# A feed-forward chunk's products grouped by width, two head groups' values issued together, and two longer distances, in a two-layer decoder trunk on one core

## The chip, the cores and the metric

The kernel runs on one core of a Trainium2 chip. The metric is the device time of one execution in microseconds (us), taken over several runs; one further execution is profiled. Five engines work side by side, each through its own queue: TensorE (PE; its weight loads are listed apart as PEld), VectorE (DVE), ScalarE (ACT), GpSimd (POOL), and SyncE (SP), which issues most DMA transfers.

## What is computed

The reference is a decoder trunk of two layers over 256 tokens of width 1024. Cut to what matters here:

```
for layer in range(2):
    x = x + 0.5 * swiglu_ffn(rms_norm(x), w_gu, w_down)      # feed-forward, width 2816
    x = x + mixer(rms_norm(x))                               # layer 0: even, layer 1: odd
    x = x + memory_cross_attention(rms_norm(x), rms_norm(mem))
    x = x + 0.5 * swiglu_ffn(rms_norm(x), w_gu2, w_down2)

def swiglu_ffn(x, w_gu, w_down):
    gate, up = jnp.split(x @ w_gu, 2, axis=-1)
    return (jax.nn.silu(gate) * up) @ w_down
```

The even mixer has eight heads of banded attention (window 128, sinks) and eight of stick-breaking attention; the odd mixer has sixteen heads whose scores get a table of distances added before the softmax. Both work with heads of 64 elements. The cross-attention has four heads of 256 over 256 memory tokens. All of it is float32.

## The kernel before

**Products.** Every weight tile of 128 x 1024 float32 elements (512 KB) is loaded into a buffer `raw`, and split into a high part `wh` (a ScalarE cast, L175) and the rest `wl` (a VectorE subtraction, L177); activations are split in the same way (`split_to`, L190 and L191). A product is then the sum of three matmuls in PSUM: high x high, high x low, low x high (`mm3`, L182 to L184). There are 10 buffers each of `wh` and `wl`, 4 of `raw`, and PSUM has 6 banks for sums (`mm`) and 2 for transposes (`tp`).

**Feed-forward.** The 2816 hidden columns are worked through in 11 chunks of 256. A chunk needs four weight tiles, and gives two results, gate and up, of 256 features x 256 tokens each. `ws_wide` makes one of the two: the weights are the stationary operand, and two banks are filled, each in eight steps over the width. A step is one matmul of 512 columns (`wh` against the high and the low half of the activations side by side, L323) and one of 256 columns (`wl` against the high half, L324), both into the same bank. ScalarE copies the second half of the bank out (L327) and VectorE adds it to the first (L328). `silu` and the product of the two results follow, and the chunk's features are split for the down projection. The first feed-forward makes chunk 0 otherwise (`ws_blocks`) and chunks 1 to 10 with `ws_wide`; the three later ones make chunks 0 and 1 token by token with `mm3` and chunks 2 to 10 with `ws_wide`. So 37 chunks, each of 32 pairs of a wide and a narrow matmul, go through it: 1184 pairs.

**The order of the attention work.** Attention is threaded between the matmuls of other projections by a clock of its own: every stretch of matmuls adds its estimated time (`tick`), and work put off with `later(delay, ...)` is issued as soon as that clock has passed its due time. The delays stand in `LAG`. `norm` is the distance from a token block's normalisation on VectorE (L231) to its transposes on TensorE; `x_p` that from the scaling of the cross-attention's weights (L452) to theirs. Where the program needs a result (`need(tag)`), what is left under that tag is issued at once. The framework under it may still move an instruction past its neighbours.

`attend` runs the attention of a list of head groups: `one(i)` makes the scores and the exponentials of group i, `share` (L452) divides by the sum, `two` transposes the weights (four transposes into a `tp` bank, L212) and copies them to SBUF (VectorE, L481), and after `LAG['pv']` `values` multiplies them with the values (L496: pairs of matmuls on one half of the output rows each). There are 6 groups in the even mixer and 12 in the odd one.

Of the kernel before, what the change touches and what calls it, by code (L numbers as in the profile page):

```python
# [27 lines left out]


LAG = {  # L30
    "norm": 5000, "silu": 5000, "pv": 3000, "head256": 2200, "band": 7500, "band_gap": 2600, "band_p": 7500,
    "put": 400, "att_norm": 4500, "band_norm": 3500, "stick_gap": 1900, "stick_u": 3200, "stick_v": 1000, "stick_o": 1300, "head64": 7000,
    "att_first": 3800, "att_gap": 3300, "att_p": 17600, "att_o": 1800, "x_s": 18000, "x_p": 4000, "x_out": 3600,
    "mem_e": 5400, "mem_o": 4600, "rs64": 2700, "rs256": 1900, "rsband": 6100,
}

# [2 lines left out]
def kernel(  # L39
# [52 lines left out]
    def later(delay, fn, tag=None):  # L92
        serial[0] += 1
        heapq.heappush(heap, (clock[0] + delay, serial[0], tag, fn))
# [8 lines left out]
    def tick(ns):  # L103
        clock[0] += ns
        if heap and not busy[0] and heap[0][0] <= clock[0]:
            dispatch()
# [40 lines left out]
    def psum():  # L147
        return mm.tile([P, 512], F32, name="mm")
# [7 lines left out]
    def work(dt=F32):  # L156
        return wk.tile([P, 512], dt, name="wk")
# [28 lines left out]
    def cols(w, o, n):  # L186
        return w[0][:, o:o + n], w[1][:, o:o + n]
# [123 lines left out]
                mm3(ps[:, b * 256:(b + 1) * 256], cols(w[k // per], o, P), xboth(k), k == 0, k == NK - 1)  # L311
                tick(330)

    def ws_wide(w, g):


        part, out = work(), work()
        for b in range(2):
            ps = psum()
            for k in range(NK):  # L320
                o = (k % 2) * 512 + g * 256 + b * P
                wh, wl = cols(w[k // 2], o, P)
                nc.tensor.matmul(ps, lhsT=wh, rhs=xs[:, :, :, k, :], start=k == 0, stop=False)  # L323
                nc.tensor.matmul(ps[:, 0:256], lhsT=wl, rhs=xh[:, :, k, :], start=False, stop=k == NK - 1)  # L324
                tick(347)
            bs = slice(b * 256, (b + 1) * 256)
            nc.scalar.copy(part[:, bs], ps[:, 256:512])  # L327
            nc.vector.tensor_tensor(out[:, bs], ps[:, 0:256], part[:, bs], op=ALU.add)  # L328
        return out


    def start(load):
# [25 lines left out]
    def ffn(w_gu, w_down, next_vec, first=False):  # L358
# [44 lines left out]
        for c in range(0 if first else 2, NF // 2):  # L403
            w = ws[0] if first and c == 0 else load_chunk(c)
            if first and c == 2:
                announce(next_vec, kept=True)
            if first and c == 0:
                pg = psum()
                ws_blocks(pg, w[0], 0, 4, by_pass=True)
                pu = psum()  # L410
                ws_blocks(pu, w[1], 0, 4)
            else:
                pg = ws_wide(w, 0)
                pu = ws_wide(w, 1)
            s = work()
            nc.scalar.activation(s, pg, AF.Silu)
            h = work()
            nc.vector.tensor_tensor(h, pu, s, op=ALU.mult)
            dh, dl = hslot(c)
            split_to(dh, dl, blocks(h, 256))  # L420
# [34 lines left out]
    def attend(groups, scores, values, gap, norm, wait, first=0.0, tag=None, ready=None):  # L455

        def one(i):
            p, nm, sink = scores(groups[i])
            n, keys = p.shape[1], p.shape[2]
            dn = sm.tile([P, 4], F32, name="dn")
            for j in range(n):
                nc.scalar.activation(p[:, j, :], p[:, j, :], AF.Exp, bias=nm[:, j:j + 1], accum_out=dn[:, j:j + 1])
            p = p.rearrange("p a b -> p (a b)")
            if sink is not None:
                nc.scalar.activation(sink, sink, AF.Exp)

            def share():
                if sink is not None:
                    nc.vector.tensor_tensor(dn[:, 0:n], dn[:, 0:n], sink, op=ALU.add)
                nc.vector.reciprocal(dn[:, 0:n], dn[:, 0:n])
                scale_heads(p, p, dn, keys)
            later(norm, share, tag)

            def two():
                ps = transpose4(p)
                pt = work()  # L480
                nc.vector.tensor_copy(pt, ps)  # L481
                if ready is None:
                    later(LAG['pv'], lambda: values(groups[i], pt), tag)
                else:
                    ready(groups[i], lambda: later(LAG['pv'], lambda: values(groups[i], pt), tag))
            later(wait, two, tag)
            if i + 1 < len(groups):
                later(gap, lambda: one(i + 1), tag)
        later(first, lambda: one(0), tag)
# [395 lines left out]
    class Memory:  # L885
# [11 lines left out]
        def values(self, arrived):  # L897

            self.v = [(slot(F32R), slot(F32R)) for _ in range(2)]

            def evac(t, c, ps):
                split_to(*[d[:, c * 512:(c + 1) * 512] for d in self.v[t]], ps)
                if t == 1:
                    arrived(c)
            project(lambda k: self.w[k * P:(k + 1) * P, 1024:2048], self.parts, evac)
# [148 lines left out]
```

## Time and profile before

| | |
|---|---|
| time, three runs | 1203.28, 1199.79, 1201.71 us; median 1201.71 |
| the profiled execution's own time | 1202.92 us |
| its span, first to last instruction | 1201.2 us |
| TensorE busy | 1189.3 us, 99% of the span |
| VectorE busy, ScalarE busy | 775.1 us (65%), 646.5 us (54%) |
| granted TensorE clock, mean | 0.999 of full speed |
| DMA | 216.70 MB, 180 GB/s |

The profiled execution took 1.7 us more than its span, before the first and after the last instruction. A row of the timeline gives the start, the duration, the engine, the line and the operation with its shapes, and in brackets how long the engine had been idle before and on whom it waited. Durations of matmuls overlap those of the next one, so that how long a matmul occupies TensorE is read from the distance between two starts, not from its duration. The clock of TensorE has two levels, 1.2 and 2.4 GHz; 1.00 in a row means 2.4.

### The profile page before, as it was taken

What the parts mean: (1) busy time and instruction counts of PE and PEld (TensorE: products, weight loads), DVE (VectorE), ACT (ScalarE), POOL (GpSimd) and SP (SyncE); (2) the same over time, 40 slices, a digit from 0 to 9 for tenths busy, and PEclk for the clock granted to TensorE, in tenths of its full rate; (3) what the DMA queues carried; (4) which work ended last, traced back from release to release, by engine and by line L of the source; (5) the groups of instructions that cost most, each with busy time, mean ns of one, the idle gap of its engine ahead of it and who ended that gap; (6) DMA issues with size and microseconds to landing.
All of it is one profiled execution on the core that took longest, in us unless ns stands there. A gap on an engine that the chain in (4) does not pass through costs nothing.

```text
span 1201.2 us, 16964 instructions
## 1 busy us (share of the span) xinstructions
PE 1189.3 (99%) x6320; PEld 998.7 (83%) x6320; DVE 775.1 (65%) x1026; ACT 646.5 (54%) x1080; POOL 63.9 (5%) x123
## 2 busy tenths in 40 slices
PE   8999999999999999999999999999999999999998
PEld 7888888986788888888888888888777888888887
DVE  6766645696777676665375765376786676667651
ACT  6656534665565466555265564265764564655540
POOL 1000000200110000000000000032000100000000
PEclk9999999999999999999999999999999999999999
DMA  8865674731454485666376657445753645665560
GB/s 253 255 195 172 218 223 131 258 105 53 145 167 144 153 266 172 191 209 210 108 250 189 193 181 274 141 158 167 230 169 121 210 143 160 202 205 188 182 192 35
DMA packets 136756, 216.70 MB, mean 180 GB/s; under 512 B 10337, under 2 KB 104161, under 8 KB 136674
## 3 DMA queue, kind: packets, MB, share of 16 engines
q1 hardware_dynamic: 136674, 215.63, 55.4%
q8 instruction: 49, 0.80, 0.3%
q14 instruction: 33, 0.27, 0.1%
HBM read 214.54 MB, written 1.05 MB: 179 GB/s over the span
## 4 chain that ended last, share of the span: by engine, by line
PE 93%; DVE 3%; DMA 2%; ACT 1%; issue 1%; POOL 0%; SPq 0%; ACTq 0%; POOLq 0%; DVEq 0%
PE mm L323 23%; PE mm L182 17%; PE mm L184 17%; PE mm L183 17%; PE mm L324 12%; PE tp L212 3%; PE mm L496 1%; DVE wl L177 1%; DMA raw<-in_xa_w_o_dram 1%; DMA raw<-in_ffn_w_gu_dram 1%; ACT wh L175 1%; PE mm L305 1%; PE mm L841 1%; DVE big L191 0%; PE mm L705 0%
## 5 line engine op out<-in xcount | busy, mean ns | idle before, releaser
L177 DVE TENSOR_TENSOR wl<-raw,wh 128x1024 fp32r<-128x1024 f32 x386 | 463.9, 1220 | 145.4 <-ACT wh L175 142.5
L175 ACT CAST wh<-raw 128x1024 fp32r<-128x1024 f32 x386 | 394.3, 1051 | 156.9 <-PE mm L184 78.7
L323 PE MATMUL mm<-xs,wh 128*128 128x512 f32 x1184 | 413.7, 394 | 0.0
L324 PE MATMUL mm<-xs,wl 128*128 128x256 f32 x1184 | 331.8, 280 | 0.0
L323 PEld LDWEIGHTS mm<-xs,wh 128*128 128x128 f32 x1184 | 221.7, 187 | 50.3
L324 PEld LDWEIGHTS mm<-xs,wl 128*128 128x128 f32 x1184 | 223.8, 189 | 0.0
L182 PE MATMUL mm<-wh,big 128*128 128x512 f32 x480 | 191.3, 399 | 0.3 <-DVE wk L713 0.3
L184 PE MATMUL mm<-wh,big 128*128 128x512 f32 x480 | 188.4, 392 | 0.0
L183 PE MATMUL mm<-wl,big 128*128 128x512 f32 x480 | 188.2, 392 | 0.0
L182 PE MATMUL mm<-wh,xs 128*128 128x512 f32 (+1 forms) x432 | 171.7, 398 | 0.0
L184 PE MATMUL mm<-wh,xs 128*128 128x512 f32 (+1 forms) x432 | 167.1, 387 | 0.0
L183 PE MATMUL mm<-wl,xs 128*128 128x512 f32 (+1 forms) x432 | 167.0, 386 | 0.0
L327 ACT COPY wk<-mm 128x256 f32<-128x256 f32 x148 | 55.0, 372 | 147.1 <-PE mm L324 146.7
L328 DVE TENSOR_TENSOR wk<-mm,wk 128x256 f32<-128x256 f32 x148 | 62.1, 421 | 94.7 <-ACT wk L327 94.7
L182 PEld LDWEIGHTS mm<-wh,big 128*128 128x128 f32 x480 | 90.5, 188 | 20.3 <-issue 2.4
L184 PEld LDWEIGHTS mm<-wh,big 128*128 128x128 f32 x480 | 90.4, 188 | 19.3 <-issue 0.3
L183 PEld LDWEIGHTS mm<-wl,big 128*128 128x128 f32 x480 | 90.6, 189 | 17.4 <-issue 0.2
L184 PEld LDWEIGHTS mm<-wh,xs 128*128 128x128 f32 x432 | 81.1, 188 | 16.9 <-issue 0.2
L182 PEld LDWEIGHTS mm<-wh,xs 128*128 128x128 f32 x432 | 81.3, 188 | 15.0 <-issue 0.5
L183 PEld LDWEIGHTS mm<-wl,xs 128*128 128x128 f32 x432 | 81.4, 188 | 14.5 <-issue 0.2
L212 PE MATMUL tp<-ident,wk 128*128 128x128 f32 x352 | 52.9, 274 | 2.4 <-DVE wk L452 0.8
L212 PEld LDWEIGHTS tp<-ident,wk 128*128 128x128 f32 x352 | 42.1, 140 | 14.2 <-issue 2.3
(148 smaller groups left out, 921.6 us busy)
## 6 DMA issues: line engine op xcount, KB each, us to landing
raw<-in_ffn_w_gu_dram SPq DMA_DIRECT2D x344, 256.0 KB, 4.2
raw<-in_ffn_w_down_dram SPq DMA_DIRECT2D x88, 512.0 KB, 4.5
raw<-in_xa_w_kv_dram SPq DMA_DIRECT2D x32, 512.0 KB, 5.4
raw<-in_od_w_in_dram SPq DMA_DIRECT2D x24, 512.0 KB, 4.5
raw<-in_ev_w_in_dram SPq DMA_DIRECT2D x18, 512.0 KB, 4.7
raw<-in_xa_w_q_dram SPq DMA_DIRECT2D x16, 512.0 KB, 4.2
raw<-in_xa_w_o_dram SPq DMA_DIRECT2D x16, 512.0 KB, 4.4
raw<-in_ev_w_out_dram SPq DMA_DIRECT2D x8, 512.0 KB, 4.1
```

Source lines behind the costliest of these rows:

```text
L175: nc.scalar.copy(wh, r)
L177: nc.vector.tensor_tensor(wl, r, f32(wh), op=ALU.subtract)
L182: nc.tensor.matmul(ps, lhsT=a[0], rhs=b[0], start=start, stop=False)
L183: nc.tensor.matmul(ps, lhsT=a[0], rhs=b[1], start=False, stop=False)
L184: nc.tensor.matmul(ps, lhsT=a[1], rhs=b[0], start=False, stop=stop)
L212: nc.tensor.transpose(ps[:, b * P:(b + 1) * P], src[:, b * P:(b + 1) * P], ident)
L305: nc.tensor.matmul(ps[:, b * 256:(b + 1) * 256], lhsT=w[k // per][x][:, o:o + P], rhs=xboth(k)[y], start=i == 0 and k == 0, stop=i == 2 an ...
L323: nc.tensor.matmul(ps, lhsT=wh, rhs=xs[:, :, :, k, :], start=k == 0, stop=False)
L324: nc.tensor.matmul(ps[:, 0:256], lhsT=wl, rhs=xh[:, :, k, :], start=False, stop=k == NK - 1)
L327: nc.scalar.copy(part[:, bs], ps[:, 256:512])
L328: nc.vector.tensor_tensor(out[:, bs], ps[:, 0:256], part[:, bs], op=ALU.add)
L496: nc.tensor.matmul(dst(h)[rows], lhsT=lhs(h), rhs=rhs(h), start=first, stop=last)
```

## The change

`ws_chunk` takes the place of two calls of `ws_wide`: it takes four banks at once, issues the 32 wide matmuls of the chunk, then the 32 narrow ones, and then evacuates the four banks. In `attend`, `two` keeps the turned weights of an even-numbered group until those of the next are there, and puts off the values of both as one piece; for the last four groups of each mixer ScalarE, not VectorE, makes the copy. `norm` goes from 5000 to 6000 and `x_p` from 4000 to 5000.

```
--- before.py
+++ after.py
@@ -28,9 +28,9 @@
 
 
 LAG = {
-    "norm": 5000, "silu": 5000, "pv": 3000, "head256": 2200, "band": 7500, "band_gap": 2600, "band_p": 7500,
+    "norm": 6000, "silu": 5000, "pv": 3000, "head256": 2200, "band": 7500, "band_gap": 2600, "band_p": 7500,
     "put": 400, "att_norm": 4500, "band_norm": 3500, "stick_gap": 1900, "stick_u": 3200, "stick_v": 1000, "stick_o": 1300, "head64": 7000,
-    "att_first": 3800, "att_gap": 3300, "att_p": 17600, "att_o": 1800, "x_s": 18000, "x_p": 4000, "x_out": 3600,
+    "att_first": 3800, "att_gap": 3300, "att_p": 17600, "att_o": 1800, "x_s": 18000, "x_p": 5000, "x_out": 3600,
     "mem_e": 5400, "mem_o": 4600, "rs64": 2700, "rs256": 1900, "rsband": 6100,
 }
 
@@ -311,22 +311,32 @@
                 mm3(ps[:, b * 256:(b + 1) * 256], cols(w[k // per], o, P), xboth(k), k == 0, k == NK - 1)
                 tick(330)
 
-    def ws_wide(w, g):
-
-
-        part, out = work(), work()
-        for b in range(2):
-            ps = psum()
+    def ws_chunk(w):
+
+
+
+        pair, outs = [(g, b) for g in range(2) for b in range(2)], []
+        banks = []
+        for g, b in pair:
+            banks.append(psum())
             for k in range(NK):
                 o = (k % 2) * 512 + g * 256 + b * P
-                wh, wl = cols(w[k // 2], o, P)
-                nc.tensor.matmul(ps, lhsT=wh, rhs=xs[:, :, :, k, :], start=k == 0, stop=False)
-                nc.tensor.matmul(ps[:, 0:256], lhsT=wl, rhs=xh[:, :, k, :], start=False, stop=k == NK - 1)
-                tick(347)
+                nc.tensor.matmul(banks[-1], lhsT=w[k // 2][0][:, o:o + P], rhs=xs[:, :, :, k, :],
+                                 start=k == 0, stop=False)
+                tick(227)
+        for (g, b), ps in zip(pair, banks):
+            for k in range(NK):
+                o = (k % 2) * 512 + g * 256 + b * P
+                nc.tensor.matmul(ps[:, 0:256], lhsT=w[k // 2][1][:, o:o + P], rhs=xh[:, :, k, :],
+                                 start=False, stop=k == NK - 1)
+                tick(120)
+            if b == 0:
+                part, out = work(), work()
+                outs.append(out)
             bs = slice(b * 256, (b + 1) * 256)
             nc.scalar.copy(part[:, bs], ps[:, 256:512])
             nc.vector.tensor_tensor(out[:, bs], ps[:, 0:256], part[:, bs], op=ALU.add)
-        return out
+        return outs
 
 
     def start(load):
@@ -410,8 +420,7 @@
                 pu = psum()
                 ws_blocks(pu, w[1], 0, 4)
             else:
-                pg = ws_wide(w, 0)
-                pu = ws_wide(w, 1)
+                pg, pu = ws_chunk(w)
             s = work()
             nc.scalar.activation(s, pg, AF.Silu)
             h = work()
@@ -458,6 +467,8 @@
 
 
 
+        turned = []
+
         def one(i):
             p, nm, sink = scores(groups[i])
             n, keys = p.shape[1], p.shape[2]
@@ -478,11 +489,22 @@
             def two():
                 ps = transpose4(p)
                 pt = work()
-                nc.vector.tensor_copy(pt, ps)
+                if i < len(groups) - 4:
+                    nc.vector.tensor_copy(pt, ps)
+                else:
+                    nc.scalar.copy(pt, ps)
+                turned.append((groups[i], pt))
+                if i % 2 == 0:
+                    return
+                both = turned[-2:]
+
+                def values_of_both():
+                    for g, weights_T in both:
+                        values(g, weights_T)
                 if ready is None:
-                    later(LAG['pv'], lambda: values(groups[i], pt), tag)
+                    later(LAG['pv'], values_of_both, tag)
                 else:
-                    ready(groups[i], lambda: later(LAG['pv'], lambda: values(groups[i], pt), tag))
+                    ready(groups[i], lambda: later(LAG['pv'], values_of_both, tag))
             later(wait, two, tag)
             if i + 1 < len(groups):
                 later(gap, lambda: one(i + 1), tag)
```

What this makes of TensorE's order at the start of the first feed-forward's chunk 1 (`xs` is the split activations, `mm` a bank). Before:

```order
L184 MATMUL mm<-xs,wl 128x256
L323 MATMUL mm<-xs,wh 128x512
L324 MATMUL mm<-xs,wl 128x256
L323 MATMUL mm<-xs,wh 128x512
L324 MATMUL mm<-xs,wl 128x256
```

And in the changed program, where the two lines have become L324 and L330:

```order
L184 MATMUL mm<-xs,wl 128x256
L324 MATMUL mm<-xs,wh 128x512 x32
L330 MATMUL mm<-xs,wl 128x256 x32
L324 MATMUL mm<-xs,wh 128x512 x32
L330 MATMUL mm<-xs,wl 128x256 x32
```

The 64 matmuls of a chunk are the same, but the width changes twice in a chunk, not at every matmul.

The second place is TensorE in the odd mixer, while it projects the memory's keys (`wh,big`). L841 is the scores of a head group, L496 its values (four pairs of matmuls on half the output rows each). Before:

```order
L184 MATMUL mm<-wh,big 128x512
L496 MATMUL mm<-wk,big 64x128 x4
L182 MATMUL mm<-wh,big 128x512
L183 MATMUL mm<-wl,big 128x512
L184 MATMUL mm<-wh,big 128x512
L841 MATMUL mm<-big 128x256 x4
L182 MATMUL mm<-wh,big 128x512
L183 MATMUL mm<-wl,big 128x512
L184 MATMUL mm<-wh,big 128x512
L496 MATMUL mm<-wk,big 64x128 x4
```

In the changed program (scores are now L863, values L518):

```order
L863 MATMUL mm<-big 128x256 x4
L182 MATMUL mm<-wh,big 128x512
L183 MATMUL mm<-wl,big 128x512
L184 MATMUL mm<-wh,big 128x512
L518 MATMUL mm<-wk,big 64x128 x8
```

The first group's values have moved behind the next scores, and stand with the second group's in one block. Over the odd mixer the 12 groups stand in 11 blocks before and in 7 in the changed program; over the even one's 6 groups in 7 blocks (one was cut in two by transposes) and in 6.

The third place is ScalarE at the end of the odd mixer's attention in the changed program (L190 is a split's cast, L175 a weight tile's):

```order
L190 CAST big<-tp 128x4x128
L495 COPY wk<-tp 128x512
L190 CAST xs<-mm 128x512
L175 CAST wh<-raw 128x1024
L190 CAST big<-tp 128x4x128
L495 COPY wk<-tp 128x512 x3
L190 CAST xs<-mm 128x512
L175 CAST wh<-raw 128x1024
```

The four L495 rows are the last groups' copies; before, they stood as L481 on VectorE.

## Rows read from the trace of the kernel before

**Rows 1.** The page: span, engines (1), granted clock by slices (2), the chain (4).

```profile
span 1201.2 us, 16964 instructions
PE 1189.3 (99%) x6320; PEld 998.7 (83%) x6320; DVE 775.1 (65%) x1026; ACT 646.5 (54%) x1080; POOL 63.9 (5%) x123
PEclk9999999999999999999999999999999999999999
PE 93%; DVE 3%; DMA 2%; ACT 1%; issue 1%; POOL 0%; SPq 0%; ACTq 0%; POOLq 0%; DVEq 0%
```

**Rows 2.** Timeline of TensorE, first feed-forward: first wide matmul, and first after the last chunk.

```profile
26.27 0.40 PE L323 MATMUL mm<-xs,wh 128*128 128x512 f32 x1
...
139.34 0.40 PE L182 MATMUL mm<-wh,big 128*128 128x512 f32 x1
```

**Rows 3.** Timeline of TensorE, second feed-forward: its 17th wide matmul, and first after the chunks.

```profile
449.04 0.40 PE L323 MATMUL mm<-xs,wh 128*128 128x512 f32 x1
...
543.34 0.39 PE L182 MATMUL mm<-wh,big 128*128 128x512 f32 x1
```

**Rows 4.** Timeline of TensorE: end of 240 wide matmuls; 24 narrow ones, then wide.

```profile
193.75 0.49 PE L212 MATMUL tp<-ident,wk 128*128 128x128 f32 x3
200.12 0.28 PE L182 MATMUL mm<-wh,xs 128*128 128x256 f32 x1
...
202.99 0.40 PE L182 MATMUL mm<-wh,xs 128*128 128x512 f32 x1
...
204.38 0.39 PE L182 MATMUL mm<-wh,xs 128*128 128x512 f32 x1
```

**Rows 5.** Timeline of TensorE around one block of values in the odd mixer.

```profile
867.89 0.40 PE L184 MATMUL mm<-wh,big 128*128 128x512 f32 x1
868.22 0.66 PE L496 MATMUL mm<-wk,big 128*64 128x128 f32 x8
868.80 0.50 PE L182 MATMUL mm<-wh,big 128*128 128x512 f32 x1
869.14 0.40 PE L183 MATMUL mm<-wl,big 128*128 128x512 f32 x1
```

**Rows 6.** Groups by line: count, busy us and mean ns; idle before, releaser.

```profile
L177 DVE TENSOR_TENSOR wl<-raw,wh 128x1024 fp32r<-128x1024 f32 x386 | 463.9, 1220 | 145.4 <-ACT wh L175 142.5
L175 ACT CAST wh<-raw 128x1024 fp32r<-128x1024 f32 x386 | 394.3, 1051 | 156.9 <-PE mm L184 78.7
L327 ACT COPY wk<-mm 128x256 f32<-128x256 f32 x148 | 55.0, 372 | 147.1 <-PE mm L324 146.7
L328 DVE TENSOR_TENSOR wk<-mm,wk 128x256 f32<-128x256 f32 x148 | 62.1, 421 | 94.7 <-ACT wk L327 94.7
L481 DVE COPY wk<-tp 128x512 f32<-128x512 f32 x18 | 12.2, 683 | 1.3 <-PE tp L212 1.3
L642 ACT COPY big<-mm 128x512 f32<-128x512 f32 x2 | 1.2, 588 | 0.3 <-PE mm L496 0.3
```

**Rows 7.** Timeline of TensorE, four single places where it waited.

```profile
373.61 0.30 PE L212 MATMUL tp<-ident,wk 128*128 128x128 f32 x1 [0.24 <-DVE wk L452]
425.15 0.30 PE L212 MATMUL tp<-ident,wk 128*128 128x128 f32 x1 [0.34 <-DVE wk L231]
902.99 0.33 PE L496 MATMUL mm<-wk,big 128*64 128x128 f32 x2 [0.55 <-DVE wk L481]
968.29 0.30 PE L212 MATMUL tp<-ident,wk 128*128 128x128 f32 x1 [0.60 <-DVE wk L452]
```

**Rows 8.** Stick-breaking attention: TensorE by windows (busy, instructions, granted clock), then its timeline.

```profile
286.00:290.00 4.00, 2.32 (x10) 1.00 0.00 0
290.00:294.00 4.00, 4.00 (x13) 0.57 0.02 4
290.36 0.63 PE L184 MATMUL mm<-wh,big 128*128 128x512 f32 x1
290.79 0.63 PE L182 MATMUL mm<-wh,big 128*128 128x512 f32 x1
```

## Prediction

> **What bounds the kernel now.** I read the page first. TensorE is busy 1189.3 of 1201.2 us, at a granted clock of nine tenths or more in all forty slices, and makes up 93% of the chain that ended last [rows 1]. So only two things shorten the time: a smaller distance between the starts of TensorE's matmuls, and fewer gaps in front of them. VectorE and ScalarE have a third and more of the span free, and work taken from them pays only where TensorE waits for it at that place. The gaps that the page counts are 1201.2 - 1189.3 = 11.9 us, part of them before the first matmul.
>
> Then I read distances between starts in the timeline, because the page's busy time hides them. In the first feed-forward 320 pairs of a wide and a narrow matmul take 139.34 - 26.27 = 113.07 us, 353.3 ns a pair [rows 2]. In the second, 272 pairs from the 17th on take 543.34 - 449.04 = 94.30 us, 346.7 ns a pair [rows 3]. The instructions and shapes are the same; the alternation has two paces, 6.7 ns apart. Runs of one width have one: 240 wide matmuls from 139.34 [rows 2] to 193.75 take 226.7 ns each, 24 narrow ones from 200.12 to 202.99 take 119.6 ns each [rows 4]. Their sum, 346.3 ns, is the faster pace of the pairs.
>
> Last I read the single places where TensorE waited [rows 7, 8], and what a block of values costs between other matmuls [rows 5].
>
> **The change part by part.**
>
> (a) Products by width. The 1184 pairs stay. If the grouped runs keep the pace of the runs above, a pair costs 346.3 to 346.7 ns whatever came before. The 320 pairs of the first feed-forward then gain 320 x 6.7 ns = 2.1 us. The three later ones start each with some 15 pairs before the pace of [rows 3] sets in; if those run at the slower pace, 3 x 15 x 6.7 ns = 0.3 us more. Against it stand the changes of width, two in each of 37 chunks. From narrow to wide the six starts after 202.99 take 1.39 us to 204.38 [rows 4], where 6 x 0.2267 = 1.36: 0.03 us. I take a price of 0.01 us a chunk, 0.4 us in all, between 0 and 37 x 0.03 = 1.1. So (a) gives 2.0 us.
> No row shows runs of the wide matmul on this strided operand. Its bound on the other side: in the slower pace a pair is 353.3, and with the narrow one at 119.6 that leaves up to 233.7 for the wide. All 1184 at that would cost 1184 x 7.0 ns = 8.3 us against 226.7. I take the pace of the runs, since the same operand reaches their sum in [rows 3].
>
> (b) Banks and buffers. Four banks are open in a chunk, and are evacuated together. The first of the four is ready three narrow runs, 3 x 8 x 0.12 = 2.9 us, before the chunk's end. The next chunk takes the two free banks first, and needs this one after two wide runs, 2 x 8 x 0.227 = 3.6 us. That leaves 6.5 us for a copy of 0.37 and an addition of 0.42 [rows 6], which may stand behind two casts of 1.05 and two subtractions of 1.22 [rows 6]: 5.3 us in all. It fits, so I cost it at nothing. The `wl` tiles come free later in a chunk, but ten buffers are 2.5 chunks of work, 2.5 x 32 x 0.347 = 27.8 us ahead. If the cover is gone, each chunk waits: 0.2 us a chunk would eat 7.4 us.
>
> (c) Values of two groups together. Around one block the start before it is 0.33 us away from it, where a wide matmul takes 0.227, and the first one behind it takes 0.34 [rows 5]: 0.10 + 0.11 us for going in and out. Inside, four pairs take 0.58 us. Two blocks made one save at least one way in and out, 0.21 us; the most is that plus half of the 0.58 us that a block takes by itself, 0.5 us. I take 0.26, near the lower end. The odd mixer loses four blocks and the even one one: 5 x 0.26 = 1.3 us, between 1.0 and 2.5.
>
> (d) Copies by ScalarE. Eight copies of 0.68 us leave VectorE, and ScalarE takes about 0.59 us for the same form from PSUM [rows 6]. None of it is on TensorE's path but where TensorE waited for such a copy: 0.55 us in front of the values at 902.99 [rows 7], which is one of the last four groups. I take 0.5, between 0 and 1.0, because a VectorE that is less loaded may shorten a neighbouring wait too. Behind the copies in ScalarE's queue stand a split's cast and weight casts; if the transposes come late, these wait, and their cover is again the ten buffers.
>
> (e) The distances. `x_p` puts 1000 on its clock, one or two more steps of three wide matmuls (0.68 us each) in front of the transposes that waited 0.24 and 0.60 us. `norm` does the same where they waited 0.34 us [rows 7]. Together 1.2 us; at least 0.6, if the splits that follow the last transposes of a cross-attention are then late for its outputs, before which the changed order has three matmuls in place of nine.
>
> (f) A clock drop. Between 286 and 290 us TensorE is busy only 2.32 of 4 us, and the next window has a granted clock of 0.57 [rows 8]: matmuls start 0.43 us apart (290.36 to 290.79), not 0.23. Some seven matmuls at 0.2 us more are 1.4 us. In the changed order three wide matmuls, 0.68 us, have moved from the band's part into this gap. The idle time of 1.68 us becomes 1.0, and I expect the clock to stay up: the 0.55 us at 902.99 brought no drop with it. Together 0.7 + 1.4 = 2.1 us, between 0 and 2.1.
>
> The sum is 2.0 + 1.3 + 0.5 + 1.2 + 2.1 = 7.1 us. The profiled execution took 1202.92 us with what lies around its span, which is 1.2 us over the median 1201.71. 1202.92 - 7.1 = 1195.8, and I forecast 1196. Against the median that is 0.5% less. A measurement of this kernel can tell about 0.3%, 3.6 us, from no change, so "faster" begins below 1198.1.
>
> **The rivals.**
>
> R1, most of it is not there. A matmul has a fixed cost beyond its columns that the order of widths doesn't touch, so (a) gives nothing; the clock drop stays, so (f) gives 0.7 at most; and of the waits in (d) and (e) half come back one step later. Then 1.3 + 0.7 + 0.9 = 2.9 us are left: 1200.0. For it speaks that the faster pace of the pairs already equals the sum of both widths, so that grouping has nothing to win wherever that pace rules [rows 3, 4]. Against it stand the first feed-forward's 113 us at the slower pace [rows 2].
> The Trainium skill (TensorE: Matmul & The Clock Gate, section "Back-to-back issue gap") gives the distance between two matmuls as the columns at 2.4 GHz plus 2.5 ns; by that a wide and a narrow one cost 215.8 + 109.2 = 325.0 ns in any order (an estimate), grouping is worth nothing, and the sum without (a) would be 5.1 us, 1197.8. The trace differs: 346.7 ns is the least that a pair takes, and the same order of the same shapes ran at two paces, so the formula of the Trainium skill does not hold the whole of this stream.
>
> R2, the other side: the wide matmul over four strided pieces in a row does not reach 226.7 ns. At the bound of (a) it costs 8.3 us where I have a gain of 2.0. With the other 5.1 us that makes 1202.92 + 8.3 - 5.1 = 1206.1, slower by 0.4%. It decides from 5.1 / 1184 = 4.3 ns a pair on: beyond that the change loses. Against it speaks [rows 3], where this operand is streamed in every second matmul at no more than the sum.
>
> R3, evacuation: 37 chunks each wait for a bank or a weight tile. At 0.3 us a chunk this costs 11 us and gives 1206.9; it decides from 7.1 / 37 = 0.19 us on. The 6.5 us against 5.3 of (b) speak against it.
>
> R4, more: the less loaded VectorE also takes away waits that I left standing, and the merged blocks reach 0.5 us each. Some 3 us more: 1192.8.
>
> **How the numbers follow.** The forecast (1193.3 to 1198.1) has a chance of 0.54, R1 0.25, R2 0.07, R3 0.05, R4 0.09. Faster by over 0.3% are the forecast and R4, 0.63; slower R2 and R3, 0.12; R1 is within 0.3%, 0.25. The range reaches from R4's side, 1191, over the forecast and R1 to 1201.5, which leaves out R2, R3 and the ends, some 2 in 10.
>
> **What would show it.** For (a): 32 wide starts in 7.25 us and 32 narrow ones in 3.84 us in every chunk, the first feed-forward's ten chunks in 110.9 us where they took 113.1. For (b): no idle time before the wide matmuls that ends on the evacuating addition. For (c): 7 blocks of values in the odd mixer, those of eight pairs near 1.0 us. For (d) and (e): the four idle times of [rows 7] gone. For (f): a granted clock of 1.00 around the stick-breaking part. Wrong would be wide starts more than 4 ns above 226.7, waits at bank changes, or a clock drop that stays or comes at a new place.

## The result and the profile after

The changed kernel takes 1218.2 us (median of six runs, 1214.65 to 1223.36) where the kernel before, on the same chip, takes 1201.82: a ratio of 1.0142, interval 1.0115 to 1.0168. It is slower by 17 us by that ratio, 16.4 by the medians; the prediction said 1196. The profiled execution took 1218.59 us. Its page, in the order of [rows 1]:

```profile
span 1216.9 us, 17014 instructions
PE 1193.6 (98%) x6320; PEld 1002.0 (82%) x6320; DVE 763.6 (63%) x1018; ACT 650.4 (53%) x1088; POOL 64.8 (5%) x123
PE 64%; DVE 15%; DMA 12%; issue 6%; ACT 2%; SPq 1%; ACTq 0%; POOL 0%; DVEq 0%; POOLq 0%
L182 PE MATMUL mm<-wh,big 128*128 128x512 f32 x480 | 194.2, 405 | 9.7 <-DVE wk L338 9.4
L338 DVE TENSOR_TENSOR wk<-mm,wk 128x256 f32<-128x256 f32 x148 | 55.9, 417 | 161.2 <-ACT wk L337 161.2
```

The chain that ended last is now only 64% TensorE; 27% of it runs through VectorE and transfers of weights. (Lines have moved: L337 is the copy that evacuates a bank and L338 the addition behind it, L327 and L328 before; L324 and L330 are the wide and the narrow matmul.) The chain of waits, first TensorE's (who waited for whom, us in total, times, longest), then ScalarE's and VectorE's:

```profile
PE mm L182 <- DVE wk L338: 9.4, 4, 2.7
PE mm L324 <- DVE wk L338: 1.6, 5, 0.6
ACT wh L175 <- DMA raw<-in_ffn_w_gu_dram: 89.6, 87, 2.3
ACT wh L175 <- DMA raw<-in_ffn_w_down_dram: 43.8, 45, 2.5
DVE wk L338 <- ACT wk L337: 161.2, 39, 5.0
DVE wl L177 <- ACT wh L175: 102.3, 96, 2.8
```

Four waits of 2.2 to 2.7 us stand in front of the four down projections, for an evacuating addition. VectorE idles 161.2 us for ScalarE's copies (94.7 before [rows 6]), and ScalarE's casts wait 133.4 us for the feed-forward's transfers; before it was 29.4 + 6.6.

Where the time went is read by stage, from the first and last starts of matmuls in the timeline. "Products" runs from the first wide matmul of a feed-forward to the first matmul of its down projection, "down" from there to that projection's 200th matmul; "layer" is what lies between that 200th matmul of a layer's first feed-forward and the first wide matmul of the next feed-forward, the attention work for the most part.

| us | before | after |
|---|---|---|
| start to the first wide matmul | 26.27 | 24.90 |
| products, four feed-forwards | 113.07, 100.25, 100.25, 100.25 | 114.30, 100.37, 101.25, 101.11 |
| down, four feed-forwards | 45.12, 45.15, 45.15, 45.15 | 49.23, 49.40, 49.69, 49.28 |
| layer 0, layer 1 | 258.63, 264.34 | 257.23, 262.54 |

The down projections lose 17.0 us, the products 3.2; the layers gain 3.2. The start's 1.4 us are put down to no edit: in the traces of this study the first wide matmul comes between 24.2 and 26.8 us, also among kernels with the same start (26.27 in before, 25.42 and 24.56 in two that change only later work), and the clock at the start differs between them (four matmuls of L305 take 1.22 us at 12.08 in the trace of before, 0.74 at 11.86 in that of after).

One of the four places, in the timeline of after:

```profile
128.00 7.53 PE L324 MATMUL mm<-xs,wh 128*128 128x512 f32 x32
135.37 4.00 PE L330 MATMUL mm<-xs,wl 128*128 128x256 f32 x32
136.71 1.05 ACT L175 CAST wh<-raw 128x1024 fp32r<-128x1024 f32 x1 [0.54 <-DMA raw<-in_ffn_w_down_dram]
139.20 0.40 PE L182 MATMUL mm<-wh,big 128*128 128x512 f32 x1
139.32 1.05 ACT L175 CAST wh<-raw 128x1024 fp32r<-128x1024 f32 x1 [1.56 <-DMA raw<-in_ffn_w_down_dram]
140.36 0.39 PE L184 MATMUL mm<-wh,big 128*128 128x512 f32 x1
141.09 1.04 ACT L175 CAST wh<-raw 128x1024 fp32r<-128x1024 f32 x1 [0.72 <-DMA raw<-in_ffn_w_down_dram]
142.04 0.64 ACT L337 COPY wk<-mm 128x256 f32<-128x256 f32 x2
142.43 0.76 DVE L338 TENSOR_TENSOR wk<-mm,wk 128x256 f32<-128x256 f32 x2 [4.05 <-ACT wk L337]
142.91 0.50 PE L182 MATMUL mm<-wh,big 128*128 128x512 f32 x1 [2.16 <-DVE wk L338]
144.91 0.63 PE L182 MATMUL mm<-wh,big 128*128 128x512 f32 x1
145.34 0.63 PE L183 MATMUL mm<-wl,big 128*128 128x512 f32 x1
```

The reader is to see ScalarE's queue. The first of the four banks is full about 2.9 us before 139.20, at 136.3. Three casts stand in front of its copy, and each waits for its transfer: 0.54 + 1.56 + 0.72 us. The copy starts at 142.04, the addition ends at 142.8, and the down projection, which had the two free banks for its first six matmuls, stops for 2.16 us. Then, by windows, what follows the stop:

```profile
139.20:143.00 3.80, 1.64 (x9) 1.04 (x7) 0.57 (x2) 2.71 (x5) 0.00 (x0) 1.00 0.56 224
143.00:147.00 4.00, 4.00 (x11) 3.14 (x12) 4.00 (x7) 2.25 (x5) 0.00 (x0) 0.60 0.34 108
```

(After the window and its length the columns are the busy time of PE, PEld, DVE, ACT and POOL with the number of instructions, the granted clock, and the DMA's share and GB/s.) TensorE's clock falls to its lower level, 1.2 of 2.4 GHz, and from 143.7 to 147.4 nine starts lie 3.65 us apart where 2.04 is the pace of wide matmuls: 1.6 us. By the distances of starts the four stops cost 2.4 to 2.9 us, and the low clock behind each of them 1.4 to 1.6: these are the 4.1 to 4.5 us that each down projection lost. The drop at 290 us [rows 8] is gone in this trace.

The delay was not there from the first chunk on. In the third feed-forward, the narrow matmuls and the first additions behind them, in its first grouped chunk and in its last:

```profile
642.06 4.00 PE L330 MATMUL mm<-xs,wl 128*128 128x256 f32 x32
644.12 0.43 DVE L338 TENSOR_TENSOR wk<-mm,wk 128x256 f32<-128x256 f32 x1 [3.11 <-ACT wk L337]
...
731.86 4.00 PE L330 MATMUL mm<-xs,wl 128*128 128x256 f32 x32
739.43 0.76 DVE L338 TENSOR_TENSOR wk<-mm,wk 128x256 f32<-128x256 f32 x2 [4.66 <-ACT wk L337]
```

The first addition starts 2.1 us after the first narrow matmul in the first of these chunks, 7.6 us in the last. From the start of the bank's last narrow matmul to the end of that addition it is 1.7 us in the first of the nine chunks, then 3.4, 4.2, 5.0, 5.7, 6.5, 6.9, 6.8 and 7.2: the delay builds up from chunk to chunk, and the down projection meets it at its largest.

### The profile page after: what moved, and what is told of

Read it like the earlier page. It is cut to its first block, busy times and chain, and to the rows that moved or that the text cites. A ratio compares the mean times of both kernels' runs of the same rounds, so it can differ in the third digit from the quotient of the medians.

```text
span 1216.9 us, 17014 instructions
## 1 busy us (share of the span) xinstructions
PE 1193.6 (98%) x6320; PEld 1002.0 (82%) x6320; DVE 763.6 (63%) x1018; ACT 650.4 (53%) x1088; POOL 64.8 (5%) x123
## 4 chain that ended last, share of the span: by engine, by line
PE 64%; DVE 15%; DMA 12%; issue 6%; ACT 2%; SPq 1%; ACTq 0%; POOL 0%; DVEq 0%; POOLq 0%
PE mm L182 17%; PE mm L184 17%; PE mm L183 17%; DMA raw<-in_ffn_w_gu_dram 7%; DVE wl L177 7%; PE mm L324 5%; DMA raw<-in_ffn_w_down_dram 4%; DVE wk L338 3%; PE tp L212 3%; PE mm L330 2%; DVE wk L427 2%; ACT wk L337 1%; ACT wh L175 1%; PE mm L518 1%; SPq L171 0%
## 5 line engine op out<-in xcount | busy, mean ns | idle before, releaser
L175 ACT CAST wh<-raw 128x1024 fp32r<-128x1024 f32 x386 | 402.3, 1052 | 294.4 <-PE mm L184 100.8
L324 PE MATMUL mm<-xs,wh 128*128 128x512 f32 x1184 | 279.4, 392 | 1.8 <-DVE wk L338 1.6
L324 PEld LDWEIGHTS mm<-xs,wh 128*128 128x128 f32 x1184 | 218.6, 188 | 49.8 <-DVE wk L338 6.0
L182 PE MATMUL mm<-wh,big 128*128 128x512 f32 x480 | 194.2, 405 | 9.7 <-DVE wk L338 9.4
L184 PE MATMUL mm<-wh,big 128*128 128x512 f32 x480 | 190.0, 396 | 0.0
L338 DVE TENSOR_TENSOR wk<-mm,wk 128x256 f32<-128x256 f32 x148 | 55.9, 417 | 161.2 <-ACT wk L337 161.2
L330 PEld LDWEIGHTS mm<-xs,wl 128*128 128x128 f32 x1184 | 146.9, 192 | 2.9
L330 PE MATMUL mm<-xs,wl 128*128 128x256 f32 x1184 | 147.8, 283 | 0.0
L190 ACT CAST big<-wk 128x512 fp32r<-128x512 f32 x38 | 23.6, 622 | 73.7 <-DVE wk L427 73.7
L218 ACT ACTIVATE junk<-x 128x512 bf16<-128x512 f32 x32 | 20.1, 628 | 61.8 <-DVE x L256 29.7
```

Of the source, the lines that this page charges most:

```text
L175: nc.scalar.copy(wh, r)
L182: nc.tensor.matmul(ps, lhsT=a[0], rhs=b[0], start=start, stop=False)
L184: nc.tensor.matmul(ps, lhsT=a[1], rhs=b[0], start=False, stop=stop)
L190: nc.scalar.copy(dh, src)
L218: nc.scalar.activation(junk, xt[:, i * 512:(i + 1) * 512], AF.Square, scale=1.0 / 32.0, accum_out=ss[:, i:i + 1])
L324: nc.tensor.matmul(banks[-1], lhsT=w[k // 2][0][:, o:o + P], rhs=xs[:, :, :, k, :], start=k == 0, stop=False)
```

## The experiments

Three accounts were tried. Theory Q: the grouped products give four banks back in one burst, whose copies stand in ScalarE's queue behind casts that wait for transfers; the subtractions behind the late additions free the arriving buffers late, so transfers and casts come later still. Rival W: weight tiles are late, because `wl` stays in use longer. Rival P: runs of one width are slower than the alternation. A ratio is that to the kernel before on the same chip, with its 95% interval; 0.1% is 1.2 us. Spans are compared by stages, because of the start's scatter.

**chunk_only**: the kernel before with the products by width, no other edit.

```diff
-                pg = ws_wide(w, 0)
-                pu = ws_wide(w, 1)
+                pg, pu = ws_chunk(w)
```

> The kernel before with the grouped chunk alone; values, copies and distances as they were. All theories: the loss is in the feed-forwards, so about 1219 to 1222 us (the changed kernel's 1218 and the 1.4 + 1.8 us that its attention stages came out shorter), with the wide matmul's wait on VectorE's additions at the start of each of the four down projections. A time near 1202 would put the loss into the attention edits.

Measured: 1221.22 us, ratio 1.0151 (1.0128 to 1.0173). The whole loss is in this edit. Its chain of waits has what that of after has, and no wait for a weight tile in the chunks:

```profile
PE mm L182 <- DVE wk L338: 9.6, 4, 2.8
PE mm L324 <- DVE wk L338: 1.5, 4, 0.5
```

But only two of its four stops, 2.76 and 2.04 us long, have a low clock behind them; those of 2.19 and 2.61 us have not, here the latter:

```profile
741.92 0.50 PE L182 MATMUL mm<-wh,big 128*128 128x512 f32 x1 [2.61 <-DVE wk L338]
742.00:746.00 4.00, 4.00 (x18) 3.30 (x19) 4.00 (x7) 2.02 (x5) 0.00 (x0) 1.00 0.40 108
```

Without the low clock a down projection lost 2.5 and 2.9 us, with it 4.7 and 3.9.

**attn_only**: the changed kernel with `ws_wide` put back.

> The attention edits and the two distances alone; the chunk's products alternate as before. From the two profiles' stages about 3 us less than before, 1198 to 1200; no wait at the down projections, and the granted clock stays up in the stick-breaking part. My prediction's terms would give 5.1 us less, 1197.

Measured: 1200.82 us, 0.998 (0.9969 to 0.9991). Products and down projections are those of before to 0.03 us; layer 0 takes 257.69, layer 1 264.71. So the attention's edits gain 2.4 us by the times, and 0.6 us by the two layers of the traces, not the 5.1 us of steps (c) to (f). One wait that the longer distances were to take away, 0.60 us at 968.29 in before [rows 7], is even longer here:

```profile
966.92 0.63 PE L212 MATMUL tp<-ident,wk 128*128 128x128 f32 x4 [1.15 <-DVE wk L452]
```

**last_wide**: the changed kernel, with each feed-forward's last chunk by `ws_wide`, which is put back beside `ws_chunk`.

```diff
...
-                pg, pu = ws_chunk(w)
+                pg, pu = ws_chunk(w) if c < NF // 2 - 1 else (ws_wide(w, 0), ws_wide(w, 1))
```

> The changed kernel, but the last chunk of each feed-forward goes through the old alternating helper, so its banks come ready one after the other. Theory Q (the evacuation stands behind weight casts in ScalarE's queue that wait for transfers, and the down projection needs its banks 4.3 us after they are ready): the four waits of 2.2 to 2.7 us and the clock drops behind them go, 1218 - 17 = 1201, and the waits of 0.2 to 0.6 us between chunks stay. Rival W (the long narrow run frees the low weight tiles late, so that weights are late): all other chunks still do that, 1210 or more.

Measured: 1206.12 us, 1.0026 (1.0013 to 1.004). The down projections are back at 45.12 us each, without a drop of the clock, while the chunks still wait (113.89, 102.19, 100.92 and 100.57 us). The 17.0 us of the down projections are thus decided by how the last chunk gives back its banks. The time is 5 us above the 1201 that theory Q gave: the chunks still lose, and the two layers take 258.45 and 263.81 us, 2.5 more than in after, which the edit doesn't explain.

**two_banks**: the changed kernel, grouped within gate and within up, two banks at a time.

```diff
-    def ws_chunk(w):
+    def ws_half(w, g):
...
-        pair, outs = [(g, b) for g in range(2) for b in range(2)], []
+        pair, outs = [(g, b) for b in range(2)], []
...
-                pg, pu = ws_chunk(w)
+                pg = ws_half(w, 0)
+                pu = ws_half(w, 1)
```

> The changed kernel, but grouped within each of the chunk's two results: 16 wide matmuls, 16 narrow ones, evacuation of two banks, then the other result. Theory Q: copies come twice a chunk, no longer in one burst of four, the waits at banks go, and the pace of single-width runs stays: 1195 to 1199. Rival P (runs of one width have a cost of their own on the chip that the alternation hides): as slow as the changed kernel, 1215 or more. Rival W: in between, 1205 to 1212.

Measured: 1199.27 us, 0.9967 (0.9952 to 0.9982): faster than before, 0.3 us above theory Q's range. Products 111.33 and 3 x 100.50 us, down projections 45.13, no wait for a bank. P falls: the runs of one width are as quick as expected.

From a bank's last narrow matmul (its start) to the end of its addition, as a mean over the 148 banks of a trace: before 1.59 us, after 5.22, chunk_only 5.06, two_banks 2.26. In two_banks the delay of a chunk's first bank falls from 7.8 us early in the first feed-forward to 1.9 and stays there; it doesn't build up. Two runs then cut one link of theory Q each, with all four banks still given back together.

**evac_dve**: the changed kernel, a bank's copy on VectorE.

```diff
-            nc.scalar.copy(part[:, bs], ps[:, 256:512])
+            nc.vector.tensor_copy(part[:, bs], ps[:, 256:512])
```

> The changed kernel, but the copy of a bank's second half in a chunk is done by VectorE instead of ScalarE; the additions follow on VectorE. Theory Q1 (the copies are late because they stand behind weight casts in ScalarE's queue that wait for their transfers): without that queue the four waits before the down projections, 9.4 us after the change, fall under 3 us, the down projections return to 45 to 46 us each from 49.3, and the time to 1201 to 1206 us. Rival Q2 (four banks given back together are too many whoever copies them, or VectorE's own queue holds them as long, since its subtractions wait for the same casts): still 6 us or more of waits there, down projections of 48 us or more, 1212 to 1220 us.

**raw6_wsp9**: the changed kernel with more room for transfers.

```diff
-    raw = ctx.enter_context(tc.tile_pool(name="raw", bufs=4))
-    wsp = ctx.enter_context(tc.tile_pool(name="wsp", bufs=10))
+    raw = ctx.enter_context(tc.tile_pool(name="raw", bufs=6))
+    wsp = ctx.enter_context(tc.tile_pool(name="wsp", bufs=9))
```

> The changed kernel with six buffers for arriving weights instead of four, and nine instead of ten for the split ones (the memory holds no more). Theory Q1 with its second half (casts wait for transfers because the arriving buffers come free late): transfers start earlier, casts wait less, copies stand less long in ScalarE's queue; the waits before the down projections fall from 9.4 us to 2 to 6, the time to 1205 to 1214 us. Rival Q2 (it is the number of banks and the burst of four copies and additions alone, whatever the transfers do): waits of 8 us or more, 1216 to 1220 us. If nine split buffers are too few, new waits of matmuls for wh or wl tiles appear in the chunks, which would be told apart by the tile they name.

Measured: evac_dve 1197.53 us, 0.996 (0.9947 to 0.9974); raw6_wsp9 1196.79 us, 0.9952 (0.9934 to 0.9971). Both beat the kernel before, and more clearly than theory Q had them. In neither is there a wait for a bank, and the down projections take 45.13 us. Their groups of the wide matmul, whose idle time was 1.8 us after the change, first evac_dve:

```profile
L324 PE MATMUL mm<-xs,wh 128*128 128x512 f32 x1184 | 276.5, 390 | 0.0
```

and raw6_wsp9:

```profile
L324 PE MATMUL mm<-xs,wh 128*128 128x512 f32 x1184 | 276.4, 390 | 0.0
```

The mean from last narrow matmul to addition is 2.01 and 1.72 us. In evac_dve the casts still wait, by its chain of waits:

```profile
ACT wh L175 <- DMA raw<-in_ffn_w_gu_dram: 54.0, 71, 2.0
ACT wh L175 <- DMA raw<-in_ffn_w_down_dram: 36.4, 36, 4.0
```

but no copy stands behind them. (These 90.4 us, where before had 36.0, also show that the casts of the grouped kernel wait even without late copies.) In raw6_wsp9 the copies stand behind casts, but these hardly wait for the feed-forward's transfers any more; this one row is all that is left of 133.4 us:

```profile
ACT wh L175 <- DMA raw<-in_ffn_w_gu_dram: 9.1, 14, 1.7
```

And the same place in its timeline: copies at 133.32 and 134.53, the down projection without a gap.

```profile
131.63 4.00 PE L330 MATMUL mm<-xs,wl 128*128 128x256 f32 x32
135.46 0.40 PE L182 MATMUL mm<-wh,big 128*128 128x512 f32 x1
...
136.62 0.39 PE L184 MATMUL mm<-wh,big 128*128 128x512 f32 x1
136.85 0.39 PE L182 MATMUL mm<-wh,big 128*128 128x512 f32 x1
```

So neither four banks at once (rival Q2) nor late casts alone make the loss; it is both in one queue. In both kernels the delay of a chunk's first bank settles, at 1.2 and 1.7 us, where in after it grows. W falls too: with fewer split buffers, nine, the matmuls of the chunks wait for none.

**before_raw6 and chunk_raw6**, the controls: the same buffers under the kernel before, and under that with the products by width alone.

> The control: the kernel before, with six buffers for arriving weights and nine split ones and nothing else. Theory Q1 (the buffers help only because they let the grouped products give their banks back in time): the kernel before has no waits in its chunks or in front of its down projections that they could take away, so its span is that of before within 2 us and the ratio 0.998 to 1.002. Rival B (the buffers are worth 5 us by themselves, and the changed kernel with them gains by them alone): 1196 to 1198 us, ratio 0.995 to 0.997.

> The kernel before with the grouped products and the same buffers (six and nine), without any edit of the attention. Theory Q1: step (a) of the prediction is whole, minus 1.9 us in the first feed-forward and plus or minus 0.1 in the others, the down projections keep their 45.1 us, and the time is 1199 to 1201.5 us (ratio 0.997 to 1.0). Rival Q2 (the buffers alone don't suffice and the attention's edits helped): waits in front of the down projections again, over 1205 us.

Measured: 1204.82 us, 1.0016 (1.0007 to 1.0025), and 1202.2 us, 0.9995 (0.9986 to 1.0004). The buffers alone gain nothing; they lose, by a new wait in layer 1 for a `wl`, with a drop of the clock behind it (267.77 us where it was 264.34). That the nine split buffers make this wait is likely but not shown; raw6_wsp9, which has them and the attention's edits, lacks it. In before_raw6's timeline and windows:

```profile
800.80 0.50 PE L183 MATMUL mm<-wl,xs 128*128 128x512 f32 x1 [1.84 <-DVE wl L177]
```

```profile
802.00:806.00 4.00, 4.00 (x14) 3.23 (x13) 3.26 (x5) 1.80 (x4) 2.77 (x4) 0.58 0.69 249
```

chunk_raw6 has this wait as well, and its layers take nearly the same time as those of before_raw6 (257.93 and 267.84 against 258.21 and 267.77). So the two show step (a) alone: products 111.12 against 113.07, and 100.36 against 100.25 three times, 1.6 us less in all. The quotient of the two ratios, 0.9979, says 2.5 us, with some 1.5 us of uncertainty (both half-widths, added in squares). The time is 0.7 us above the range given, the ratio within it.

**lag_only, merge_only and copies_only**: one of the attention's edits each, on the kernel before.

> The kernel before with the two longer distances alone. The prediction's steps (e) and (f) hold that x_p and norm take 0.6 to 1.2 us from three waits. The attention edits together took 2.1 us off the span, 1.5 of them before the first feed-forward, where only the distance norm can act. Theory D (the distances do most of it): the first feed-forward's products begin at 24.7 to 24.9 us instead of 26.27, and the span is 1.2 to 2.0 us shorter; the half clock near 290 us stays, since the band's matmuls are not moved. Rival M (the start is moved by the merged values or the copies, and the distances give nothing or lose): products begin at 26.2, span within 0.5 us of 1201.2.

> The kernel before with the values of two groups together alone (VectorE copies all turned weights, the distances are those of before). Step (c) of the prediction: 5 x 0.26 = 1.3 us less, between 1.0 and 2.5. Theory M1: the two attention layers, 258.6 and 264.3 us, are shorter by 1.0 to 1.3 us together, and the half clock near 290 us goes, because the merging moves three wide matmuls into the gap there. Rival M2 (a block of values waits for the second of its two groups, and what the joining saves is lost in such waits): the sum of the two layers changes by less than 0.4 us or grows.

> The kernel before with the copies of the last four groups' turned weights by ScalarE alone. Step (d) of the prediction: minus 0.5 us, between 0 and 1.0. Theory C1 (the copies are what takes away the half clock near 290 us, which stays with the distances alone and with the merged values alone): no half clock there and the first attention layer shorter by about 1.5 us, 257 us. Rival C2 (only all three edits together move enough): the half clock stays, the two attention layers change by less than 0.6 us each, and the time is that of before within 1 us.

| | time, ratio (interval) | layer 0, layer 1 (before 258.63, 264.34) | low clock near 290 us |
|---|---|---|---|
| lag_only | 1200.83 us, 0.9988 (0.9976 to 1.0001) | 257.32, 263.43 | stays |
| merge_only | 1202.89 us, 1.0007 (0.9996 to 1.0019) | 259.06, 264.97 | stays |
| copies_only | 1202.50 us, 1.0004 (0.9994 to 1.0014) | 258.72, 263.91 | gone |

The distances do what (e) said: the waits at 373.61, 425.15 and 968.29 us [rows 7], 1.18 us together, are gone from lag_only's trace, and the layers are shorter by 1.31 + 0.91 us, about 1.9 us of it at these three places. That the products also begin earlier there was not the distance, as theory D had it: merge_only, which lacks it, begins at 24.56. The merged values alone lose 1.06 us in the layers (M2): the values' wait for a VectorE copy, 0.55 us in before [rows 7], takes 1.8 us, and the three waits of (e) grow from 1.18 us to 0.83 + 0.74 + 1.01 = 2.58.

```profile
PE mm L506 <- DVE wk L483: 1.8, 1, 1.8
```

The copies alone take away the low clock near 290 us, as C1 said, but the layer is no shorter (C2): the granted clock is 1.00 there, and TensorE is busy 2.87 of the 4 us between 286 and 290. It's the copies throughout: the six traces without this edit have the drop near 290 us, the eight with it don't.

```profile
286.00:288.00 2.00, 1.77 (x8) 0.79 (x6) 0.61 (x2) 1.67 (x5) 0.47 (x1) 1.00 0.00 0
288.00:290.00 2.00, 1.10 (x4) 0.66 (x4) 1.35 (x3) 0.61 (x3) 0.94 (x2) 1.00 0.00 0
```

**raw6_nomerge**: raw6_wsp9 with each group's values by themselves.

> The changed kernel with six and nine buffers, but each head group's values by themselves as before. If the merging by itself loses (merged alone, the two attention layers grew by 1.06 us together), this one is faster than the changed kernel with those buffers: 1195.5 to 1196.5 us, its attention layers below 257.3 and 262.97 us. If the merging gains what step (c) says once its neighbours are moved too, this one is slower by 1.0 to 1.3 us: 1197.5 to 1198.5 us.

Measured: 1199.74 us, 0.9974 (0.9962 to 0.9985), above both ranges given. Its layers take 257.63 and 263.52 us, those of raw6_wsp9 257.30 and 262.97: here the merging gains 0.9 us. The ratios, 0.9974 and 0.9952, lie 2.6 us apart, with as much uncertainty; the traces start 2.2 us apart, at 26.56 and 24.33 us. The waits of (e) are in neither trace, so the merging has nothing to lose there. The sign of step (c) depends on the distances or copies that come with it.

## Why the prediction was wrong

**The step that failed is (b)**, "I cost it at nothing", and with it rival R3 had too small a chance. The step set 5.3 us of work against 6.5 us until the next chunk needs the bank, and was wrong in three ways.

- It counted the work in front of the copy, not the waiting in front of that work, and took the delay as the same in every chunk. In the rows at 136.71 to 142.04 three casts stand in front of the copy with 2.82 us of waiting for transfers, where the step has two casts without any. A late addition makes the subtraction behind it late, and with it the buffer for the next transfer, so that the delay builds up, from 1.7 us to 7.2 in the third feed-forward; the casts' waits rise from 36.0 us before to 133.4. A bank's addition ends 5.22 us after its last narrow matmul starts, as a mean, and in the first feed-forward's last chunk 6.0 to 6.7 us. That the mean lies next to the step's 5.3 is chance, as it is the mean of a delay that grows. Where the trace of before has the casts waiting for transfers 29.4 us already, 5.3 us of 6.5 was no cover.
- It looked only at the next user in the steady loop. Behind the last chunk the next user is the down projection, which takes a bank after every three matmuls at first: its third bank is wanted 1.4 us after its start, which leaves 2.9 + 1.4 = 4.3 us, less than the step's own 5.3. That this doesn't fit could have been seen from the kernel's order and [rows 4, 6] alone. The slack to the next chunk, 6.5 us, was used up too, in nine later chunks: their third bank came 0.3 to 1.0 us late, which makes most of the 4.8 us that the products take longer than in raw6_wsp9 (the waits list shows 1.6 of them as idle time).
- It gave a wait its own length as its price. Behind all four stops in after stands a low clock that costs another 1.4 to 1.6 us, as [rows 8] had shown at another place; in chunk_only it stands behind two of four.

R3 named the evacuation, but spread over 37 chunks, and gave 1206.9. The loss is 17 us in four places that it didn't look at, and 4.8 in the chunks, of which (a) gives 1.6 back.

**(a)** was right: 1.6 us by stages where it had 2.0. The grouped runs keep the expected pace: in the rows from 24.90 of the timeline of after 32 wide starts take 7.28 us (7.25 was said), and the ten chunks 111.13 us (110.9) wherever their four banks come free in time. R2 falls. The formula that R1 takes from the Trainium skill (TensorE: Matmul & The Clock Gate, section "Back-to-back issue gap") is given there for an isolated matmul, not for a stream like this one, so that the difference which R1 finds doesn't contradict it.

**(c)** was 1.3 us; 0.9 is what it brought in the one pair of kernels that differ by it alone beside the other edits, and by itself it lost 1.06.

**(d)** was 0.5 us. The wait at 902.99 [rows 7] is gone in after, but the values at 914.70 us wait 0.75 and those at 266.69 us 0.33 us for ScalarE's copies: the wait changed its engine, as R1 had it for half of such waits.

**(e)** was 1.2 us. It is met in lag_only and in after, where the three waits are gone, but not in attn_only, which waits 0.20 and 1.15 us at two of them in spite of the longer distances.

**(f)** was right that the clock stays up near 290 us, and on what the low clock costs there: the same fifteen matmuls take 4.61 us from 289.76 in before and 3.07 from 290.21 in copies_only, 1.5 us where (f) had 1.4. It was wrong that the layer keeps this. The copies alone take the drop away, and copies_only's layer 0 is as long as before: two waits of (e), at 373.61 and 425.15 us [rows 7], grow there from 0.24 and 0.34 us to 0.44 and 0.75, a new wait for a copy takes 0.33 us at 262.52, and the rest wasn't traced.

The layers together gain 3.2 us in after and 3.3 in evac_dve where the sum of (c) to (f) was 5.1. The three edits one by one give 2.2 - 1.06 + 0.34 = 1.5 us and in attn_only 0.6. The steps were added up as if each stood alone, but what is saved in front of a wait for VectorE can come back as a longer wait, as merge_only and copies_only show. Of the 2.8 us between the layers of attn_only and evac_dve, 1.8 us arise at the two waits for L452 in attn_only, counted matmul by matmul; why these come back in one kernel and not in the other stays open.

With the evacuation cured in any of three ways the kernel comes near to where the prediction put it: 1199.27, 1197.53 and 1196.79 us, by the ratios 4.0, 4.8 and 5.8 us less than before. So its sum of 7.1 us was 1 to 3 us too large, and what sank it was the one edit that was priced at nothing.

The Trainium skill (Perfetto Trace Analysis, section "Matmuls") says that independent groups of matmuls should go round the banks, so that the evacuation of one lies beside the matmuls of the next. The traces agree where ScalarE makes the copies and four buffers take the arrivals: two banks at a time, 0.9967, four given back at the chunk's end, 1.0142. With the copies on VectorE or six arriving buffers, four at the chunk's end did as well, 0.996 and 0.9952.

## What to carry to other kernels

When a change collects releases into a burst, price the latest one through the queue that it stands in, with the waits of what is queued ahead, and against every next user, the one behind the loop's last iteration first. If the copies that free a bank share an engine with casts that wait for transfers, each can feed the other's delay: look whether the delay grows from one iteration to the next. Moving the copies, deeper buffers for arrivals, or smaller bursts each stopped it here. A regrouping of matmuls that is worth 1.6 us was decided by a copy of 0.37 us on another engine. And gains in front of a wait don't add up until the wait is gone.

## What was not expected of the hardware

- A stop of 2.16 us in front of a down projection was followed by the lower clock from 143.7 to 147.4 us, and so was one of 1.84 us before 800.80 us in before_raw6; but stops of 2.19 and 2.61 us at the same places of chunk_only were not. The length of the stop alone does not decide it, and what does was not found. At the low level wide matmuls start 0.42 to 0.43 us apart.
- The alternation of a wide and a narrow matmul has two paces, 353.3 and 346.7 ns a pair [rows 2, 3]. The slower one holds throughout the first feed-forward of every kernel that alternates, and in the alternating last chunk of all four feed-forwards of last_wide (11.31 us for 32 pairs). In before's second one it gives way to the faster pace behind two transposes (L397) at 448.47 us. Runs of one width have one pace, 111.13 us for 320 pairs, 347.3 ns. What sets the slower pace was not tried.
- The first wide matmul came between 24.2 and 26.8 us. raw6_wsp9 and raw6_nomerge, equal up to there, differ by 2.2 us; the granted clock from 15 to 18 us is 1.00 in the one and 0.50 in the other. In a kernel of 1200 us this is 0.2%, as much as most of these edits.
